# A decoder layer's first norm: its weight row by a 512 KB transfer instead of two products, and one run of warm-up products

## The chip, the cores and the metric

The kernel runs on one core of one Trainium2 chip. A core has five engines that run side by side and wait for each other by semaphores: TensorE (PE: matrix products, with a path of its own for loading weights, PEld), VectorE (DVE), ScalarE (ACT), GpSimd (POOL) and SyncE (SP), which here only issues transfers. Sixteen DMA engines move data between the main memory and the on-chip memory SBUF; TensorE writes to PSUM, a smaller memory that DVE and ACT can read.

The metric is the device time of one execution in microseconds, lower is better. The kernel before takes 733.38 us (median of 3 runs, 732.4 to 733.74).

## The reference

One layer of a hybrid decoder on 512 tokens of width 1024, all in float32. Cut to the frame, with the three mixers left as calls:

```python
def rms_norm(x, g):
    return x * lax.rsqrt(jnp.mean(x * x, axis=-1, keepdims=True) + EPS) * g

def reference(x, norm_mix, w_in, ..., w_out, norm_ffn, w_ffn1, w_ffn2):
    h = rms_norm(x, norm_mix[0])
    proj = h @ w_in[0]                        # 1024 -> 2974 columns, split into the parts below
    qkv_a, z_a, b_a, a_a, q_b, kv_b, gate_b, u_c = split_columns(proj)
    y_a = gdn_mixer(...)                      # convolution, gated delta rule in chunks of 64, 6 heads
    y_b = nsa_mixer(...)                      # compressed, selected and windowed attention, 6 heads
    y_c = pool_mixer(...)                     # causal means over 2, 4, 8 and 16 tokens
    x = x + concat(y_a, y_b, y_c) @ w_out[0]
    h = rms_norm(x, norm_ffn[0])
    return x + square(relu(h @ w_ffn1[0])) @ w_ffn2[0]
```

The change lies wholly in the first line: `norm_mix[0]` is a row of 1024 weights that every token's row of `x` is multiplied by.

## The kernel before

**Tiling.** The 512 tokens are four tiles of 128 rows, `x0` to `x3` (128 partitions by 1024 columns, 512 KB each). Every float32 product of the large projections is made of three products of rounded parts: a tile is split into `hi` (rounded, by ACT) and `lo` (the rest, by DVE), and `hi*hi`, `hi*lo` and `lo*hi` are summed in PSUM.

**The first stage** (the first 24 us or so) makes the normalised and transposed `hTh` and `hTl` out of `x`. It has these steps for tile `i`, each a function whose calls stand in the order in which they are wanted:

- `load_x(i)` (L200) loads the tile. `dma_a(0)` and `dma_a(1)` (L206) load the 286 columns of `w_in` that are projected first, in two halves of four row blocks each, `raw`.
- `norm_sq(i)` (L153): ACT squares the tile and sums each row into `ss`.
- `norm_root(i)` (L159): the reciprocal square root of the 128 sums by three Newton steps: three small DVE instructions (L163 to L165), then six more, on DVE for tile 0 (L171, L172) and on POOL for tiles 1 to 3 (L168, L169).
- `norm_b(i)` (L175): DVE forms `scr = x * r * gmix` in two halves of 512 columns (L179), `gmix` being the weight row on all 128 partitions; TensorE transposes the eight 128 by 128 blocks against the identity (L183).
- `norm_c(i)` (L186): ACT and DVE split the transposed blocks into `hTh` (L191) and `hTl` (L192).
- `hi_a`, `lo_a` (L210, L215) split the loaded columns of `w_in` (ACT, L213; DVE, L218), and `proj_a` (L250) multiplies with them (L257 to L259).

The calls from L307 to L331 give the order of all of this. `kp` (`keep_in_program_order`) marks the instructions whose order on their engine is the written one, so none of them overtakes another there: the DVE part of `norm_root(1)`, for one, is written ahead of `lo_a(0)`, which is written ahead of `norm_c(0)`.

**The weight row and the warm-up** (L224 to L240). The row is loaded as one row on one partition, `grow` (4 KB, issued by ACT). A column of ones, `onep` (1 by 128), times each half of `grow` gives a 128 by 512 PSUM tile whose rows are all that half: the two tiles `gmix`, which stay in two of the eight PSUM banks until `norm_b(3)`. Around these two products stand two runs of eight products of the identity with itself, whose result nobody reads: they keep TensorE busy before there is work for it.

**The order elsewhere.** SP issues nearly all loads, one after the other in the order of its program. After the first stage there is no written order for the engines: a scheduler plays the program through with its own estimate of durations and puts each instruction where its inputs are there first. So a change at the start can change the order of instructions that it doesn't touch. The delta rule (`gdn_solve` with products of L804; `gdn_step` with L884, L888, L901, L909), the projections (L429), the compression (L592 to L612) and the start of the attention are interleaved in this way. The last stage (the MLP) is one long run of products.

Of the kernel before, what the change touches and what calls it, by code (L numbers as in the profile page):

```python
# [9 lines left out]
F32 = mybir.dt.float32  # L10
# [10 lines left out]
P = 128  # L21
T = 512
D = 1024
# [14 lines left out]
def trunk_kernel(ctx, tc, x, norm_mix, w_in, conv_w, a_log, dt_bias, gdn_norm, nsa_q_norm, nsa_k_norm,  # L38
                 cmp_pos, cmp_w1, cmp_w2, pool_w, pool_scale, w_out, norm_ffn, w_ffn1, w_ffn2, out):
    nc = tc.nc  # L40
    V, S, G, PE, SY = nc.vector, nc.scalar, nc.gpsimd, nc.tensor, nc.sync

    def pool(name, bufs, side="left", space=None, reuse="tile"):
        kw = {} if space is None else {"space": space}
        return tc.tile_pool(name=name, bufs=bufs, side=side, reuse_waits=reuse, **kw)
# [11 lines left out]
    def banks(*ids):  # L57

        c = [0]

        def get():
            b_ = ids[c[0] % len(ids)]
            c[0] += 1
            return bank.tile([P, 512], F32, tag=f"b{b_}", name=nm("ps"))

        return get
# [4 lines left out]
    pp_, ps_, pc_ = banks(3, 6), banks(3), banks(6)  # L71

    def ctile(shape, dt, name):
        return cst.tile(shape, dt, tag=name, name=name)
# [12 lines left out]
    xin = xes.enter_context(pool("xin", 1, side="right"))  # L87

    ident = ctile([P, P], F32, "ident")
# [6 lines left out]
    def bc(ap, name, n, tmp=True):  # L96
        t = xin.tile([P, n], F32, tag=name, name=name) if tmp else ctile([P, n], F32, name)
        SY.dma_start(t, ap.partition_broadcast(P))
        return t
# [51 lines left out]
    kp = tc.keep_in_program_order  # L151
# [48 lines left out]
    def load_x(i):  # L200
        t = xin.tile([P, D], F32, tag=f"x{i}", name=f"x{i}")
        SY.dma_start(t, x[0, ts(i, P), :])
        xw[i] = t
        xt[i] = [t[:, ts(b, T)] for b in range(2)]
# [16 lines left out]
                slab_a[c].append(t_[:, k])  # L221

    xt, xw, ra, nr, nps = {}, {}, [], {}, {}
    one1 = xin.tile([1, 1], F32, tag="one1", name="one1")  # L224
    V.memset(one1, 1.0)
    S.activation(one1, one1, AF.Square)
    load_x(0)
    grow = xin.tile([1, D], F32, tag="grow", name="grow")
    S.dma_start(grow, norm_mix[0:1, :])
    onep = xin.tile([1, P], F32, tag="onep", name="onep")  # L230
    V.memset(onep, 1.0)
    wps = pn()
    gmix = [pp_() for _ in range(2)]
    for n_ in (8, None, 8):
        if n_:
            for _ in range(n_):
                kp(PE.matmul(wps[:, 0:P], ident, ident, start=True, stop=True))
        else:
            for b in range(2):
                kp(PE.matmul(gmix[b], onep, grow[:, ts(b, T)], start=True, stop=True))  # L240
    for i in range(2):
        ra.append(dma_a(i))
        load_x(i + 1)
# [1178 lines left out]
```

## Time and profile before

| | |
|---|---|
| median of 3 runs | 733.38 us (732.4 to 733.74) |
| the profiled execution | 730.48 us |
| its span, first to last instruction | 728.6 us |
| TensorE busy | 701.8 us, 96% of the span |
| VectorE, ScalarE, GpSimd busy | 557.3, 387.5, 167.4 us |
| mean granted TensorE clock | 0.988 |

All times of rows are microseconds from the start of the span. Busy time counts from an instruction's start to its modelled end. A row of the timeline shows in square brackets how long the engine had been idle before it and what ended that. The granted clock of 1.00 is 2.4 GHz and 0.50 is 1.2 GHz.

### The profile page before, as it was taken

The page shows a single profiled execution, that of the slowest core. Times are in us where ns is not written, and L with a number is a line of the kernel's source. Part 1 is how long each engine was busy: PE and PEld are TensorE (multiplying, and loading weights), DVE is VectorE, ACT ScalarE, POOL GpSimd, SP SyncE. Part 2 cuts the span into 40 slices and gives each one's busy share as a digit, 9 for nine tenths or more (in the row PEclk, how much of TensorE's full clock was granted, in tenths as well). Part 3 has the DMA queues.
Part 4 walks back from the last instruction along what each step waited for, and adds up shares of the span by engine and source line. Part 5 has one row for each costly group of instructions (what it writes and reads, how often), then busy time and mean ns, then how long its engine had stood idle before and what let it go on. Part 6 is the DMA issues. An engine that isn't in the chain of part 4 may idle for free.

```text
span 728.6 us, 13287 instructions
## 1 busy us (share of the span) xinstructions
PE 701.8 (96%) x5147; PEld 574.5 (79%) x5147; DVE 557.3 (76%) x1061; ACT 387.5 (53%) x768; POOL 167.4 (23%) x257
## 2 busy tenths in 40 slices
PE   8999999999999999899899999999999999999997
PEld 6888887887988776666678878888888888888885
DVE  6778998878686678877646798997968586796836
ACT  5455745664653558468734844545453544544430
POOL 6810012312132110000020140505032050504123
PEclk9999999998999999899999999999999999999999
DMA  6242213141400500323011152415051333312103
GB/s 221 66 131 87 74 44 89 31 110 44 126 22 16 232 1 30 95 88 109 0 38 51 59 173 94 139 58 167 14 166 58 117 115 108 124 47 70 57 1 115
DMA packets 49780, 61.67 MB, mean 85 GB/s; under 512 B 5479, under 2 KB 42549, under 8 KB 49718
## 3 DMA queue, kind: packets, MB, share of 16 engines
q1 hardware_dynamic: 48852, 60.64, 26.5%
q8 instruction: 40, 0.66, 0.4%
q10 hardware_dynamic: 866, 0.20, 0.1%
q14 instruction: 22, 0.18, 0.1%
HBM read 58.73 MB, written 2.10 MB: 83 GB/s over the span
## 4 chain that ended last, share of the span: by engine, by line
PE 71%; DVE 16%; ACT 4%; DMA 4%; issue 3%; POOL 2%; SPq 0%; DVEq 0%; ACTq 0%; POOLq 0%
PE ps L143 17%; PE ps L144 17%; PE ps L145 17%; PE ps L429 6%; PE ps L804 2%; PE ps L1144 2%; DMA raw<-in_w_ffn_dram 2%; PE ps L1130 1%; DVE lw L135 1%; DVE lo L135 1%; DMA raw<-in_w_out_dram 1%; PE ps L592 1%; PE ps L1105 1%; DVE lwo L135 1%; DVE bl L1298 1%
## 5 line engine op out<-in xcount | busy, mean ns | idle before, releaser
L144 PE MATMUL ps<-h2l,hw 128*128 128x512 f32 (+1 forms) x280 | 104.9, 375 | 0.1
L145 PE MATMUL ps<-h2h,lw 128*128 128x512 f32 (+1 forms) x280 | 104.8, 375 | 0.0
L143 PE MATMUL ps<-h2h,hw 128*128 128x512 f32 (+1 forms) x280 | 104.1, 375 | 0.0
L143 PE MATMUL ps<-bh,ah 128*128 128x512 f32 x224 | 88.3, 394 | 0.7 <-DVE x L1391 0.7
L144 PE MATMUL ps<-bl,ah 128*128 128x512 f32 x224 | 88.2, 394 | 0.0
L1305 POOL TENSOR_TENSOR al<-gF,ah 128x512 fp32r<-128x512 f32 x24 | 35.0, 1459 | 230.0 <-ACT ah L1304 190.5
L145 PE MATMUL ps<-bh,al 128*128 128x512 f32 x224 | 84.4, 393 | 0.0
L1391 DVE TENSOR_TENSOR x<-ps,x 128x512 f32<-128x512 f32 x112 | 73.1, 683 | 14.4 <-PE ps L145 14.4
L1298 DVE TENSOR_TENSOR bl<-w2r,bh 128x1024 fp32r<-128x1024 f32 x40 | 57.8, 1448 | 7.2 <-ACT bh L1297 7.2
L144 PEld LDWEIGHTS ps<-h2l,hw 128*128 128x128 f32 x280 | 52.6, 188 | 10.4 <-DVE h2l L1269 0.3
L145 PEld LDWEIGHTS ps<-h2h,lw 128*128 128x128 f32 x280 | 52.6, 188 | 10.2
L143 PEld LDWEIGHTS ps<-h2h,hw 128*128 128x128 f32 x280 | 52.3, 188 | 10.0
L1297 ACT CAST bh<-w2r 128x1024 fp32r<-128x1024 f32 x40 | 41.8, 1047 | 32.6 <-PE ps L145 32.0
L1305 POOL TENSOR_TENSOR al<-gS,ah 128x512 fp32r<-128x512 f32 x32 | 54.1, 1707 | 17.3 <-ACT ah L1304 17.3
L135 DVE TENSOR_TENSOR lo<-raw,hi 128x512 fp32r<-128x512 f32 (+1 forms) x76 | 43.9, 601 | 14.9 <-ACT hi L134 12.5
L134 ACT CAST hi<-raw 128x512 fp32r<-128x512 f32 (+1 forms) x76 | 37.0, 518 | 28.4 <-DMA raw<-in_w_in_dram 12.2
L143 PEld LDWEIGHTS ps<-bh,ah 128*128 128x128 f32 x224 | 42.1, 188 | 11.2 <-ACT ah L1304 0.9
L145 PEld LDWEIGHTS ps<-bh,al 128*128 128x128 f32 x224 | 42.1, 188 | 9.7
L144 PEld LDWEIGHTS ps<-bl,ah 128*128 128x128 f32 x224 | 42.1, 188 | 9.7
L134 ACT CAST hw<-raw 128x1024 fp32r<-128x1024 f32 x32 | 32.2, 1047 | 27.1 <-PE ps L144 23.5
L135 DVE TENSOR_TENSOR lw<-raw,hw 128x1024 fp32r<-128x1024 f32 x32 | 39.1, 1256 | 8.4 <-ACT hw L134 8.2
L144 PE MATMUL ps<-hTl,hi 128*128 128x512 f32 x104 | 41.3, 397 | 0.0
(375 smaller groups left out, 1687.1 us busy)
## 6 DMA issues: line engine op xcount, KB each, us to landing
raw<-in_w_ffn_dram SPq DMA_DIRECT2D x32, 512.0 KB, 3.8
w2r<-in_w_ffn_dram SPq DMA_DIRECT2D x32, 512.0 KB, 4.5
raw<-in_w_in_dram SPq DMA_DIRECT2D x24, 256.0 KB, 2.9
raw<-in_w_in_dram SPq DMA_DIRECT2D x36, 128.0 KB, 2.6
x<-in_x_dram SPq DMA_DIRECT2D x8, 512.0 KB, 6.3
raw<-in_cmp_w_dram SPq DMA_DIRECT2D x32, 128.0 KB, 2.1
raw<-in_w_out_dram SPq DMA_DIRECT2D x8, 512.0 KB, 4.5
out_dram<-x SPq DMA_DIRECT2D x8, 256.0 KB, 2.0
```

The lines of the kernel that those rows point to most:

```text
L134: {"A": S.copy, "V": V.tensor_copy, "G": G.tensor_copy}[e[0]](hi[:, k], r)
L135: {"V": V, "G": G}[e[1]].tensor_tensor(lo[:, k], r, f32v(hi[:, k]), ALU.subtract)
L143: PE.matmul(ps, ah, bh, start=start, stop=False, **kw)
L144: PE.matmul(ps, ah, bl, start=False, stop=False, **kw)
L145: PE.matmul(ps, al, bh, start=False, stop=stop, **kw)
L429: PE.matmul(ps[:, ts(i, 256)], a_[:, k, ts(2 * b + i, P)], w_, start=(k == 0 and n_ == 0 and i == 0), stop=(k == KC - 1 and n_ == 2 and i ...
L804: PE.matmul(ps[halves[p], ts(s_, 64)], lhsT(halves[p], s_), rhs(halves[p], s_), start=True, stop=True)
L1144: PE.matmul(acc[0:64 if b == 2 else P, i * P:(i + m) * P], v_ if b == 2 else v_.rearrange("p c d -> p (c d)"), p_[:, c * P:(c + m) * P], s ...
L1297: S.copy(hi, src)
L1298: V.tensor_tensor(lo, src, f32v(hi), ALU.subtract)
L1305: G.tensor_tensor(lo, src, f32v(hi), ALU.subtract)
L1391: V.tensor_tensor(x2[i][:, cs], acc[bk, t_], x2[i][:, cs], ALU.add)
```

## The change

The weight row is loaded straight onto all 128 partitions: `bc`, a helper that the kernel already has for small rows, issues one transfer from SP whose source is read 128 times (128 rows of 4 KB, 512 KB), right behind the load of `x0`. `gmix` is now two halves of that SBUF tile. The load of `grow` by ACT, the two products and the two PSUM banks go. `onep` becomes a 128 by 128 tile of ones, set by DVE as its first instruction, and the warm-up is one run of 22 products of it with itself.

```diff
+    onep = xin.tile([P, P], F32, tag="onep", name="onep")
+    V.memset(onep, 1.0)
     one1 = xin.tile([1, 1], F32, tag="one1", name="one1")
     V.memset(one1, 1.0)
     S.activation(one1, one1, AF.Square)
     load_x(0)
-    grow = xin.tile([1, D], F32, tag="grow", name="grow")
-    S.dma_start(grow, norm_mix[0:1, :])
-    onep = xin.tile([1, P], F32, tag="onep", name="onep")
-    V.memset(onep, 1.0)
+    gm_b = bc(norm_mix[0], "gm_b", D)
+    gmix = [gm_b[:, ts(b, T)] for b in range(2)]
+
     wps = pn()
-    gmix = [pp_() for _ in range(2)]
-    for n_ in (8, None, 8):
-        if n_:
-            for _ in range(n_):
-                kp(PE.matmul(wps[:, 0:P], ident, ident, start=True, stop=True))
-        else:
-            for b in range(2):
-                kp(PE.matmul(gmix[b], onep, grow[:, ts(b, T)], start=True, stop=True))
+    for _ in range(22):
+        kp(PE.matmul(wps[:, 0:P], onep, onep, start=True, stop=True))
```

The line numbers of the changed kernel are 5 lower than those of the kernel before from here on.

SP's program at its start, the kernel before (`x` with a number is a token tile, `raw` the columns of `w_in`, `vrow` small rows):

```order
L202 DMA x_90<-in_x_dram 128x1024
L127 DMA raw_119<-in_w_in_dram 128x4x268
L127 DMA raw_119<-in_w_in_dram 128x4x18
L202 DMA x_122<-in_x_dram 128x1024
L127 DMA raw_126<-in_w_in_dram 128x4x268
L127 DMA raw_126<-in_w_in_dram 128x4x18
L202 DMA x_129<-in_x_dram 128x1024
```

and the changed one:

```order
L202 DMA x_92<-in_x_dram 128x1024
L98 DMA gm_b<-in_norm_mix_dram 128x1024
L127 DMA raw_121<-in_w_in_dram 128x4x268
L127 DMA raw_121<-in_w_in_dram 128x4x18
L202 DMA x_124<-in_x_dram 128x1024
L127 DMA raw_128<-in_w_in_dram 128x4x268
L127 DMA raw_128<-in_w_in_dram 128x4x18
L202 DMA x_131<-in_x_dram 128x1024
```

One transfer of the size of a token tile stands between `x0` and all that follows on SP; nothing else moves there.

TensorE's program some 169 us into the span, where its order first differs behind the start, the kernel before (L603 belongs to the compression, L804 and L612 to the solve and the compression, L888 and L901 to one step of the delta rule's scan, L429 to a projection):

```order
L603 MATMUL ps_1985<-id_146,hid_2674 128x64 x2
L888 MATMUL ps_3098<-S_3096,kr 64x64
L804 MATMUL ps_2108<-LT_880,kr 64x64 x12
L804 LDWEIGHTS L_1401
L804 MATMUL ps_2169<-W_556,L_1401 64x64
...
L612 MATMUL ps_1985<-w_2672,hh_2678 64x64 x2
L888 MATMUL ps_3098<-S_3096,kr 64x64 x2
L554 MATMUL ps_3793<-ident,X_3737 128x128
```

and the changed one:

```order
L883 MATMUL ps_3100<-S_3098,kr 64x64 x3
L598 MATMUL ps_1987<-id_148,hid_2676 128x64 x2
L799 MATMUL ps_2110<-LT_882,kr 64x64 x12
L799 LDWEIGHTS L_1403
L799 MATMUL ps_2171<-W_558,L_1403 64x64
...
L896 MATMUL ps_3100<-vn_3107,qr 64x64 x3
L607 MATMUL ps_1987<-w_2674,hh_2680 64x64 x2
L424 MATMUL ps_3832<-hi_3833,hTh 128x256
```

The three products of the scan step (L888, here L883) now stand together and ahead of those of the compression, and the next ones of the scan (L901, here L896) follow a solve round later. From here to the first attention head's values, at about 313 us of the span before, the order of TensorE, DVE, ACT and POOL differs in many places; before and after that stretch it is the same instruction by instruction, but for the lines of the diff.

## Rows read from the trace of the kernel before

**Rows 1.** The page: busy time by engine, share of the span, instructions.
```profile
PE 701.8 (96%) x5147; PEld 574.5 (79%) x5147; DVE 557.3 (76%) x1061; ACT 387.5 (53%) x768; POOL 167.4 (23%) x257
```
**Rows 2.** Windows: length, busy PE, PEld, DVE, ACT, POOL, clock, DMA share, GB/s.
```profile
0.00:24.00 24.00, 19.90 (x118) 16.22 (x119) 15.67 (x39) 12.99 (x26) 16.83 (x75) 1.00 0.53 170
24.00:166.00 142.00, 139.36 (x1404) 116.69 (x1403) 121.38 (x299) 82.95 (x188) 30.12 (x65) 1.00 0.31 83
166.00:314.00 148.00, 138.97 (x1740) 116.28 (x1740) 110.81 (x324) 83.72 (x219) 26.61 (x44) 0.94 0.22 71
```
**Rows 3.** Chain that ended last, first 24 us: start, length, what.
```profile
9.06 0.07 DVE ss L163
...
14.08 1.41 DVE scr L179 x2
...
21.84 0.73 DVE scr L179
```
**Rows 4.** Timeline: start, length, engine, line, what, idle before and its end.
```profile
6.48 1.14 ACT L213 CAST hi<-raw 128x1144 fp32r<-128x1144 f32 x1 [0.95 <-DMA raw<-in_w_in_dram]
...
7.77 1.06 ACT L156 ACTIVATE sq<-x 128x1024 f32<-128x1024 f32 x1 [0.15 <-DMA x<-in_x_dram]
...
8.97 0.15 DVE L163 TENSOR_SCALAR ss<-ss 128x1 f32<-128x1 f32 x1
```
**Rows 5.** Windows of the transfers: length, clock, DMA share, GB/s.
```profile
10.00:11.00 1.00, 1.00 1.02 407
```
**Rows 6.** Windows and packets while the small rows are spread over the partitions.
```profile
12.40:13.00 0.60, 1.00 0.25 61
...
DMA packets 53, 0.04 MB, mean 61 GB/s; under 512 B 5, under 2 KB 53, under 8 KB 53
...
13.40:14.40 1.00, 1.00 0.08 20
```
**Rows 7.** Groups by line and form, DVE: busy, mean ns, idle before.
```profile
L179 DVE SCALAR_TENSOR_TENSOR scr<-x,r,ps 128x512 f32<-128x512 f32 x8 | 5.6, 743 | 1.0 <-POOL r L169 0.9
...
L500 DVE SCALAR_TENSOR_TENSOR acc<-th,acc 128x512 f32<-128x512 f32 x9 | 6.2, 688 | 1.1 <-ACT th L499 1.0
...
L1373 DVE TENSOR_TENSOR gS<-gF 128x512 f32<-128x512 f32 x8 | 12.0, 1504 | 0.0
```
**Rows 8.** Timeline, POOL and DVE, around the roots of tiles 1 and 3.
```profile
9.42 1.35 DVE L218 TENSOR_TENSOR lo<-raw,hi 128x1144 fp32r<-128x1144 f32 x1
9.60 1.39 POOL L168 TENSOR_SCALAR rs<-r,ss 128x1 f32<-128x1 f32 x1 [1.74 <-DVE r L165]
...
18.38 1.41 DVE L179 SCALAR_TENSOR_TENSOR scr<-x,r,ps 128x512 f32<-128x512 f32 x2 [0.33 <-POOL r L169]
...
18.76 0.26 POOL L169 TENSOR_SCALAR r<-rs,r 128x1 f32<-128x1 f32 x1
...
20.37 0.26 POOL L169 TENSOR_SCALAR r<-rs,r 128x1 f32<-128x1 f32 x1
...
20.56 1.34 DVE L192 TENSOR_TENSOR hTl<-ps,hTh 128x512 fp32r<-128x512 f32 x2 [0.78 <-ACT hTh L191]
```
**Rows 9.** Timeline: the warm-up, the first transposes, SP's next load, its use.
```profile
1.78 3.78 PE L237 MATMUL ps<-ident 128*128 128x128 f32 x16 [1.78 <-POOL ident masks.py:199]
...
7.43 2.05 PE L237 MATMUL ps<-ident 128*128 128x128 f32 x16
...
9.32 1.04 PE L183 MATMUL ps<-ident,scr 128*128 128x128 f32 x8
...
13.54 1.25 SPq L127 DMA_DIRECT2D raw<-in_w_in_dram  x2
...
24.14 1.14 ACT L134 CAST hi<-raw 128x512 fp32r<-128x512 f32 x2
```
**Rows 10.** Windows, PE alone: length, busy, clock, DMA share, GB/s.
```profile
170.00:176.30 6.30, 5.93 (x69) 0.50 0.07 14
...
293.00:302.00 9.00, 6.66 (x40) 1.00 0.46 120
```

## The prediction, made before the changed kernel was run

> **What bounds the kernel now.** I read the busy times first: TensorE is busy 96% of the span [rows 1], so what a change is worth is what it does to the stretches in which TensorE is not fed. The windows by stage come next [rows 2]. From 24 to 166 us TensorE is busy 139.4 of 142 us: a delay at the start goes through this stretch undiminished, since nothing there waits long enough to take it up. From 166 to 314 us it is idle 9.0 us of 148 and the clock averages 0.94. In the first 24 us, where the change lies, it is idle 4.1 us, and much of what counts as busy is warm-up. What sets the end there is seen in the chain of waits [rows 3]: not products, but the run square, root, `scr`, next root on ACT, DVE and POOL, tile after tile, up to the last `scr` at 21.84; TensorE starts its unbroken run after the transposes of that. The timeline shows the link that matters here [rows 4]: ACT's square of `x1` starts at 7.77, after 0.15 us of waiting for the transfer, and DVE takes its sum at 8.97, while `scr` of tile 0 ends on DVE at 9.06 [rows 3, 4]. The two arrive together, so a later `x1` has no slack to hide in.
>
> **The transfer.** `gm_b` is 128 rows of 4 KB, 524,288 bytes, issued second on SP, ahead of the columns of `w_in` and of `x1`. The DMA engines are full in this stretch: with the same 4 KB rows they carry 407 GB/s at a share of 1.02 [rows 5], so whatever stands behind `gm_b` comes 524,288 / 407,000 = 1.29 us later. The trace has no spread of that size, so I bound it. Below: nothing, if the engines found room elsewhere; the share of 1.02 speaks against that. Above: the spread of a small row of 768 bytes runs at 61 GB/s [rows 6], which would make it 8.6 us. But in those 0.6 us 53 packets start at a share of only 0.25, and the 256-byte rows a little later make 20 GB/s at 0.08 [rows 6]: 88 and 78 packets per us. The pace there goes by packets and not by bytes, and 128 packets at 88 per us are 1.45 us. I take 1.3 us, with 0 and 8.6 kept as ends.
>
> **What it delays.** `raw` of the first half lands just ahead of 6.48 [rows 4], now 7.78; ACT's 1.14 us on it end at 8.92. `x1` is there at 7.77 + 1.3 = 9.07, its sum at 8.97 + 1.3 = 10.27. Behind that sum on DVE stand, in written order, the rest of DVE's part of tile 1's root, `lo_a(0)` and `hTl` of tile 0; POOL's part of the root waits for it too, so TensorE's first projection and `scr` of tile 1 (14.08 [rows 3]) move with it: +1.3 us. `x2`, `x3` and the second half of `w_in` are later by the same 1.3 us as their users. Their users were not waiting for them, so they add nothing. `gm_b` itself stands ahead of `raw` and so lands before 7.78. `scr` of tile 0 starts at 9.06 - 1.41 = 7.65 now; even if it waited for 7.78 it would be done by 9.2, and DVE has nothing to do after it until 10.27. So its landing is hidden. The small rows and the next `w_in` load (issued at 13.54, used at 24.14 [rows 9]) hide behind the stage.
>
> **What it saves.** The two products and the load of `grow` were done when the root was, so taking them away moves no start of `scr`. What stays of it: `scr` now reads both tensors from SBUF. With one in PSUM a half takes 743 ns; a line of the same kind with both in SBUF takes 688 [rows 7]. Five halves lie on the chain behind the late sum (two of tile 1, two of tile 2, the first of tile 3): 5 x 0.055 = 0.3 us off.
>
> **DVE against POOL.** A DVE instruction with two SBUF inputs and a POOL instruction get in each other's way: POOL's step at 9.60 takes 1.39 us and ends with DVE's `lo_a(0)`, begun at 9.42, while the same kind of step takes its normal time beside `scr` of tile 2 (0.26 us at 18.76) as long as that reads PSUM [rows 8]. After the change it doesn't. Held back for all of `scr` from 18.76, POOL's root of tile 3 would end some 1.04 us later than now (20.37 + 0.26 = 20.63), at 21.67; the last `scr` is behind `hTl` of tile 2, which ends at 20.56 + 1.34 = 21.90 [rows 8]. That cover is thin but holds. The other way round, DVE may wait for a POOL step: between 0 and, by a 512-column line that runs beside POOL all the time (1504 ns for some 690 [rows 7]), 2 x 0.8 = 1.6 us. Only a few 0.3 us steps meet `scr` here, so I take 0.2 us.
>
> The Trainium skill (SBUF — State Buffer, section "SBUF: two separate sides") states this as a lock: a DVE instruction with two SBUF inputs and a GpSimd instruction exclude each other for the whole instruction. The trace agrees at 9.60 [rows 8]. By this rule taken strictly, a POOL step that runs when `scr` is due holds it for the step's 0.3 us, and the sum below would be 1.3 in place of 1.2.
>
> **The warm-up.** Now: 16 passes in 3.78 us, that is 0.236 each, later 16 passes in 2.05, 0.128 each [rows 9]; that is the half and the full clock, though the windows give 1.00 for both. TensorE starts at 1.78 because it waits for the identity; the ones are set by DVE, which is free then, so it starts sooner, I guess at 1.1. 22 products are 44 passes: if the clock rises at about the same time (5.5), 19 slow and 25 fast ones, 4.5 + 3.2 us, an end at 8.8; as the first half of `scr` is ready at 7.65 + 0.74 = 8.4, the transposes come 0.5 us sooner than at 9.32 [rows 9]. It is worth nothing, because `hTl` of tile 0 now stands on DVE behind the late sum. It has a price instead: TensorE has almost nothing to do from about 9.8 (8.8 + 1.04, end of the transposes) to 12.1 (end of `lo_a(0)`, 9.42 + 1.35 + 1.3 [rows 8]). I cost that at 0 and treat a falling clock as a rival.
>
> **The order from 166 to 314 us.** It differs there on four engines, by the scheduler's own estimate. Both orders hold the same instructions, so the price is a difference of waits. Before, the stretch loses 9.0 us to idle time and 148 x 0.06 = 8.9 us to the clock [rows 2]. I can't tell from the order which one waits less: the three products of a scan step come together and earlier, which helps the chain of the scan, but the waits ahead of the compression stay and less independent work stands between two scan steps. The largest single event of the stretch is 6.3 us at half clock [rows 10], worth 3.2 us; one more or one fewer of these bounds the term, -3.2 to +3.2, and I take 0, in the middle.
>
> **Sum.** 1.3 - 0.3 + 0.2 + 0 + 0 = +1.2 us on the profiled execution: 730.48 becomes 731.7, its span 729.8. The profiled execution lies 2.9 us under the median of the runs, 733.38; the same +1.2 there gives 734.6.
>
> **Rivals.**
> 1. The new order waits less: one half-clock spell of the size in [rows 10] goes, -3.2 + 1.2 = -2.0: 731.4. For it: the scan runs ahead. Against: nothing in the change aims at it. 17%.
> 2. The new order waits more, slower than forecast: +3.2 + 1.2 = +4.4, 737.8. 18%.
> 3. The clock falls in the idle spell between warm-up and first projection. For it: in the kernel before, 9.0 us in which TensorE is busy 6.7 stand before another half-clock spell [rows 10]. Against: the first 24 us hold idle spells as well and products kept full speed. Its price: if 13 of the first projection's 24 products run at half speed and lose what a pass lost in [rows 9], 0.236 - 0.128 = 0.11 us each, that is 1.4 us, of which the wait for `lo_a(1)`, later as well, hides a part, I take 0.4: +1.0, so 735.6. 10%. The Trainium skill (TensorE: Matmul & The Clock Gate, section "HAM oscillation") has the rule behind this: gaps without products put the engine back to half rate, and the next work starts slow. No row here shows it in this place.
> 4. The spread is slow: at the 61 GB/s of [rows 6] `x1` comes 8.6 us later and, as `scr` of tile 0 waits too, all follows: +8.6 - 0.3 + 0.2 = +8.5, 741.9. Against: its pace goes by packets. 7%.
> 5. The delay is not there: `x1` comes no later, or the waits of 166 to 314 us take it up, 733.4, no change. 10%.
>
> **How the numbers follow.** 38% is left for the forecast, 734.6, whose own range is 733.9 to 736.0 (the transfer 1.3 to 1.45, the lock 0 to 1.6, small shifts of order). What a measurement can tell from no change is about 0.2%, 1.47 us: from 731.9 to 734.85. The forecast case lies at that edge, and I split it evenly, 19 and 19. Slower: these 19, 16 of rival 2 and 7 of rival 3 (the rest of both being smaller than priced), and the 7 of rival 4: 49%. Faster: 13 of rival 1, and 2 of rival 5 where some gain is left: 15%. The same: the remaining 36%. The range reaches from 731.0, below the first rival, to 739.0, above the second, and leaves out the fourth.
>
> **What would show it.** Right: ACT's square of `x1` starts near 9.1 after waiting for its transfer, DVE is idle before the sum of tile 1 until 10.3, the last `scr` starts near 23.0, and the 24 to 166 us stretch is as full as before. The halves of `scr` take about 690 ns where POOL is idle. Wrong: a square of `x1` at 7.8; a `scr` of tile 0 that waits for `gm_b`; products of the first projection 0.24 us apart; or a difference that arises behind 166 us, in the idle time or the clock, and outweighs the start.

## The result, and the profile after

The changed kernel takes 724.61 us (median of 5 runs, 724.29 to 725.93), the kernel before in the same job 733.38 us (728.6 to 735.64): a ratio of 0.9896, 95% interval 0.987 to 0.9922. In a second job the same two kernels gave 0.992 (0.9899 to 0.9941). The forecast was 734.6, slower; the range began at 731.0. The profiled execution takes 724.29 us, its span is 722.5 us.

The page and the windows of the changed kernel, columns as in [rows 1] and [rows 2]:

```profile
PE 696.9 (96%) x5155; PEld 573.0 (79%) x5155; DVE 554.8 (77%) x1061; ACT 386.4 (53%) x768; POOL 170.6 (24%) x257
...
0.00:24.00 24.00, 19.73 (x112) 18.09 (x113) 13.51 (x35) 11.75 (x21) 14.99 (x54) 0.93 0.59 189
24.00:166.00 142.00, 139.13 (x1374) 116.92 (x1374) 121.12 (x295) 83.11 (x192) 33.17 (x85) 1.00 0.30 81
166.00:314.00 148.00, 140.42 (x1820) 117.06 (x1817) 114.75 (x339) 88.11 (x229) 27.51 (x44) 0.99 0.24 76
```

Against [rows 2] two windows moved. The first 24 us now hold a spell at a lower clock (0.93); in 166 to 314 us the clock is 0.99 in place of 0.94, and 80 more products fit in; but that window does not hold the same work in both. To see where the 6.2 us of the profiled executions come from, the instructions of DVE and ACT were paired between the two traces by source line and count, and the start in one trace subtracted from that in the other. The changed kernel is 2.4 us behind at 24 to 40 us, 1.8 behind at 140 to 160, 6.2 ahead at 320, and 6.1 ahead at the end. So the start lost time, as forecast, and one stretch won 7.9 us. That 2.4 us become 1.8 is no sign of slack in between: a second trace of the kernel before (e5 below) gains 0.7 us on the first over the same work.

**The start.** The timeline of the changed kernel, in the order of [rows 4]:

```profile
4.82 1.06 ACT L156 ACTIVATE sq<-x 128x1024 f32<-128x1024 f32 x1 [2.52 <-DMA x<-in_x_dram]
...
8.52 1.15 ACT L213 CAST hi<-raw 128x1144 fp32r<-128x1144 f32 x1 [2.55 <-DMA raw<-in_w_in_dram]
...
9.81 1.06 ACT L156 ACTIVATE sq<-x 128x1024 f32<-128x1024 f32 x1
...
10.99 0.15 DVE L163 TENSOR_SCALAR ss<-ss 128x1 f32<-128x1 f32 x1 [1.49 <-ACT sq L156]
...
19.25 1.29 DVE L192 TENSOR_TENSOR hTl<-ps,hTh 128x512 fp32r<-128x512 f32 x2 [1.17 <-ACT hTh L191]
...
20.23 0.26 POOL L169 TENSOR_SCALAR r<-rs,r 128x1 f32<-128x1 f32 x1
...
20.91 1.42 DVE L179 SCALAR_TENSOR_TENSOR scr<-x,r,gm_b 128x512 f32<-128x512 f32 x2
...
21.08 1.30 POOL L168 TENSOR_SCALAR rs<-r,ss 128x1 f32<-128x1 f32 x1 [0.58 <-DVE r L165]
...
22.84 0.34 POOL L168 TENSOR_SCALAR rs<-r,ss 128x1 f32<-128x1 f32 x1
...
24.39 1.41 DVE L179 SCALAR_TENSOR_TENSOR scr<-x,r,gm_b 128x512 f32<-128x512 f32 x2
```

The chain of waits that ended last, in the same stretch (start, length, what, as in [rows 3]):

```profile
2.73 7.00 DMA x<-in_x_dram
...
9.81 1.16 ACT sq L156 x2
...
24.09 0.27 POOL r L169
...
24.39 0.76 DVE scr L179
```

The cast of the first columns of `w_in` waits for its transfer until 8.52 (6.48 before, [rows 4]) and keeps ACT until 9.67. `x1` lands at 2.73 + 7.00 = 9.73, and its square starts 0.08 us behind that, at 9.81 (7.77 before). The timeline shows no wait there because ACT had been free for 0.14 us only, but the chain goes by the transfer. The sum of tile 1 comes at 10.99 (8.97), the last `scr` at 24.39 (21.84, [rows 3]). TensorE in the same stretch, and one window of it (columns as in [rows 10]):

```profile
1.12 8.13 PE L235 MATMUL ps<-onep 128*128 128x128 f32 x44 [1.12 <-DVE one L227]
...
9.08 1.13 PE L183 MATMUL ps<-ident,scr 128*128 128x128 f32 x8
...
11.48 0.40 PE L252 MATMUL ps<-hi,hTh 128*128 128x286 f32 x1 [1.27 <-ACT hTh L191]
...
12.85 0.40 PE L253 MATMUL ps<-lo,hTh 128*128 128x286 f32 x1 [0.97 <-DVE lo L218]
...
14.20:17.50 3.30, 3.30 (x16) 0.50 0.12 32
```

After the transposes TensorE has nothing to do but one product until 12.85, and from about 14.2 to 17.6 it runs at 1.2 GHz.

**166 to 314 us.** The stretch between the same instructions is 166 to 314 us in the kernel before and 167.76 to 307.85 in the changed one:

```profile
167.76:307.85 140.09, 132.51 (x1738) 110.77 (x1739) 109.17 (x327) 83.38 (x219) 27.51 (x44) 0.99 0.23 74
```

With [rows 2] beside it: 148.0 us became 140.1; TensorE's busy time fell from 138.97 to 132.51 (6.5 us), its idle time from 9.0 to 7.6 (1.5 us). The work is the same, so the busy time fell because less of it ran at half clock: 17.1 us of the stretch before, 3.4 us in the changed kernel, in the clock of the two traces. The timeline of TensorE at the first place where the order differs and at a later one, some of the rows with a wait in front, first the kernel before and then the changed one:

```profile
167.02 0.38 PE L804 MATMUL ps<-TT,R 64*64 64x64 f16 x12 [0.49 <-DVE R L849]
...
167.82 0.39 PE L429 MATMUL ps<-hi,hTh 128*128 128x256 f32 x1 [0.43 <-DVE qks L542]
...
169.18 0.91 PE L603 MATMUL ps<-id,hid 128*128 128x64 f32 x4 [0.43 <-ACT hid L600]
...
229.46 0.38 PE L804 MATMUL ps<-TT,R 64*64 64x64 f16 x12 [1.39 <-DVE R L849]
```

```profile
164.59 0.38 PE L799 MATMUL ps<-TT,R 64*64 64x64 f16 x12 [0.30 <-DVE R L844]
...
171.22 0.45 PE L607 MATMUL ps<-w,hh 128*64 128x64 f32 x4 [0.35 <-DVE hh L603]
...
227.09 0.92 PE L799 MATMUL ps<-X,LT 64*64 64x64 f32 x24 [0.51 <-DVE TT L853]
...
228.40 0.91 PE L799 MATMUL ps<-LT,kr 64*64 64x64 f32 x24 [0.39 <-DVE LT L860]
```

Before, three waits stand within 2.6 us, and the clock is halved right behind them; a single wait of 1.39 us at 228 stands ahead of another half-clock spell. In the new order the waits at these two places are shorter and further apart, and in this trace no spell follows until 287 us.

### The profile page after: what moved, and what is told of

The parts are those of the page before. It is cut to its first block, busy times and chain, and to the rows that moved or that the text cites. A ratio compares the mean times of both kernels' runs of the same rounds, so it can differ in the third digit from the quotient of the medians.

```text
span 722.5 us, 13307 instructions
## 1 busy us (share of the span) xinstructions
PE 696.9 (96%) x5155; PEld 573.0 (79%) x5155; DVE 554.8 (77%) x1061; ACT 386.4 (53%) x768; POOL 170.6 (24%) x257
## 4 chain that ended last, share of the span: by engine, by line
PE 71%; DVE 16%; ACT 4%; DMA 4%; issue 3%; POOL 1%; SPq 0%; DVEq 0%; ACTq 0%; POOLq 0%
PE ps L143 17%; PE ps L144 17%; PE ps L145 17%; PE ps L424 5%; PE ps L799 2%; PE ps L1139 2%; PE ps L1125 1%; DMA raw<-in_w_in_dram 1%; PE ps L587 1%; DVE lw L135 1%; DMA raw<-in_w_ffn_dram 1%; DMA x<-in_x_dram 1%; PE ps L1100 1%; DVE bl L1293 1%; DVE lwo L135 1%
## 5 line engine op out<-in xcount | busy, mean ns | idle before, releaser
L1386 DVE TENSOR_TENSOR x<-ps,x 128x512 f32<-128x512 f32 x112 | 72.9, 681 | 10.6 <-PE ps L145 10.5
L1299 ACT CAST ah<-gS 128x512 fp32r<-128x512 f32 x32 | 19.8, 621 | 45.1 <-DVE gS L1368 24.5
```

What stands on the lines that cost most here:

```text
L1299: S.copy(hi, src)
L1386: V.tensor_tensor(x2[i][:, cs], acc[bk, t_], x2[i][:, cs], ALU.add)
```

## The experiments

All kernels below differ from one of the two in the lines shown and in nothing else that behaves differently (where the loop of the kernel before is changed, the spreading products read `onep[0:1, :]`, the same row). Behind the start each has the order, on all engines, of the kernel that is named with it: the number, the place or the operand of the warm-up products is enough to make the scheduler choose another order. Theory A: the order of 166 to 314 us made the gain, and the transfer only costs. Theory B: the transfer and the warm-up made it. Theory C: half-clock spells come and go by execution. Times are medians; ratios are to the kernel before in the same job, with 95% intervals.

**The same order with the other start.** The start of the kernel before, with the changed kernel's order:

```diff
-    for n_ in (8, None, 8):
+    for n_ in (10, None, 8):
```

> The start of the kernel before (row of weights on one partition, two spreading products, identity warm-up), with 10 + 8 instead of 8 + 8 warm-up products. Behind the start its order is that of the changed kernel, on every engine. Theory A (the order of 166 to 314 us made the gain, the transfer only costs): the changed kernel's 724.6 less the 1.8 us by which its start is behind at 160 us, 722.8; one half-clock spell or none in 166 to 314 us. Theory B (transfer and warm-up make the gain): as before, 733.4. Theory C (half-clock spells come and go by execution, whatever the order): anywhere between 723 and 735, its spells not those of the changed kernel.

The changed kernel with the order of the kernel before (the tile of ones and its setting by DVE, no longer used, go too, so TensorE starts at 1.78 as before):

```diff
-        kp(PE.matmul(wps[:, 0:P], onep, onep, start=True, stop=True))
+        kp(PE.matmul(wps[:, 0:P], ident, ident, start=True, stop=True))
```

> The changed kernel with one thing different: its 22 warm-up products multiply the identity and not the tile of ones. Behind the start its order is that of the kernel before, on every engine. Theory A: 733.4 + 1.8 (start) = 735.2, with three or four half-clock spells in 166 to 314 us, the long one near 170 us among them. Theory B: 724.6 to 726. Theory C: anywhere between 723 and 737.

Measured: 723.62, ratio 0.9893 (0.9864 to 0.9923), and 733.3, ratio 1.0019 (1.0 to 1.0038). The gain went with the order and not with the transfer: theory B fell. In the second trace the half-clock spells are those of the kernel before, each about 3.4 us later, as its start is. Windows inside these four spells, the kernel before and then the changed start with the old order (length, busy PE, clock, DMA share, GB/s):

```profile
169.50:176.20 6.70, 6.33 (x66) 0.50 0.08 19
230.90:234.20 3.30, 3.10 (x14) 0.50 0.00 0
289.00:292.20 3.20, 3.13 (x11) 0.50 0.47 164
302.60:305.90 3.30, 3.30 (x9) 0.50 0.33 134
```

```profile
172.90:179.60 6.70, 6.28 (x69) 0.50 0.07 15
234.30:237.60 3.30, 3.15 (x14) 0.50 0.00 0
292.30:295.70 3.40, 3.33 (x12) 0.50 0.53 154
306.00:309.30 3.30, 3.30 (x9) 0.50 0.27 108
```

Theory C in its plain form fell with them.

**One product more or less; four less; ones for the identity.** The kernel before with `(8, None, 9)`, `(8, None, 7)`, `(4, None, 8)` in the same line, and with the 128 by 128 tile of ones as the operand of its warm-up. Four more orders.

> The kernel before with one more warm-up product (8 + 9), which ends before the transposes begin and so delays nothing. Behind the start its order is a third one, which differs from both kernels in some 680 of TensorE's 5550 entries. Theory A: another time than 733.4 by more than 1.5 us, its sign unknown, made behind 166 us. Theory B: 733.4, within 0.7.

> The kernel before with one warm-up product less (8 + 7). Behind the start its order is a fourth one (some 610 of TensorE's entries differ from before, 710 from the changed kernel). Theory A: a time of its own again, different from that of the run with one more by over 1.5 us as likely as not, and the difference arises behind 166 us. Theory B: 733.4, within 0.7.

> The kernel before with 4 + 8 instead of 8 + 8 warm-up products. A fifth order behind the start, the nearest to that of the kernel before so far (some 260 of TensorE's entries differ). Theory A (the order decides): a time between the two kernels or beyond them, within 2 us of 731.4 if only the differing entries near 170 us matter little; its start may lose up to 1 us where the clock has not risen in time. Theory B (the start decides): 731.4 to 732.4.

> The kernel before with one part of the change alone: the warm-up (8, the two spreading products, 8) multiplies a 128 by 128 tile of ones set by DVE, the row is spread by products as before. A sixth order behind the start (some 500 of TensorE's entries differ from before, 620 from the changed kernel). Theory A: a time of its own between 722 and 738, made in 166 to 314 us. Theory B (the transfer makes the gain): 731.4 within 0.7; if the operand of the warm-up made it: 724.

Measured: 731.6, 1.0001 (0.9972 to 1.0031); 737.69, 1.0074 (1.0051 to 1.0096); 735.94, 1.0051 (1.0023 to 1.0079); 733.83, 1.0021 (0.9995 to 1.0047). One warm-up product taken away, which can only let TensorE go on sooner, made the kernel 0.74% slower; in its trace 3.4 us of that arise in the stretch, and 3.1 us at the start. (The expectation of one product more called it free. It is not: the warm-up stands in front of the first transposes, which begin at 9.32 in [rows 9] though half of their `scr` is there at 8.4.) Of the nine-product kernel theory A had expected a time of its own; its stretch was 2.1 us faster, but its start 4.2 us behind (below), so its time came out as before's. For the nearest order (`4, None, 8`) theory A had allowed 2 us; it was 4, of which its trace has 2.1 in the stretch and 2.3 at the start. The last one shows that the clock is not all of it:

```profile
166.00:314.00 148.00, 136.25 (x1776) 0.97 0.23 72
```

This is TensorE's window in the kernel with the ones: a better clock than the 0.94 of [rows 2], yet 148.00 - 136.25 = 11.75 us idle in place of 9.0, and the stretch 1.0 us slower.

**The kernel before, two more traces.** Unchanged.

> The kernel before, unchanged, for a second trace of it. Its executions differ in mean granted clock (0.984 to 0.997) and in time (730 to 737). Theory A1 (the old order loses by its half-clock spells): an execution with fewer such spells in 166 to 314 us is faster by half of what they no longer last, so with 7 instead of 17 us of them by 5 us. Theory A2 (the old order loses by what its engines wait for one another, and the clock falls because TensorE waits): the time stays within 1.5 us of 730.5 whatever the clock, and the idle time of TensorE in the stretch grows by what the spells give back.

> The kernel before, unchanged, a third trace. As for the second one: theory A1 5 us faster for 10 us less of half clock, theory A2 the same time within 1.5 us and more idle time of TensorE in place of the slow time.

Measured: 730.09 and 734.23 us. Neither execution had few enough spells to part A1 from A2. The second lacks the last spell of the kernel before; across that place it makes up 1.3 us on the first trace (paired instructions: 4.9 us behind at 280 to 300, 3.6 past it). Where a spell of 6.8 us stood in place of one of 3.4, or beside none, in two traces of one kernel (the runs f6 and g2 below), it cost 1.7 and 2.5 us more. So a microsecond at half clock cost some 0.36 to 0.5 us here, an estimate from three places. The stretch of the kernel before has 17.1 us of it and that of the changed kernel 3.4: 4.9 to 6.8 of the 7.9 us are clock, by this estimate, the rest shorter waits. No run kept the old order and its waits and changed the clock alone; that split stays an estimate.

The second trace showed something else, which the profile of the forecast had not: its start is 3.8 us behind that of the first, in the same kernel.

```profile
1.79 3.78 PE L237 MATMUL ps<-ident 128*128 128x128 f32 x16 [1.79 <-POOL ident masks.py:199]
5.50 3.78 PE L240 MATMUL ps<-grow,onep 1*128 1x512 f32 x4
9.21 3.78 PE L237 MATMUL ps<-ident 128*128 128x128 f32 x16
12.78 1.74 PE L183 MATMUL ps<-ident,scr 128*128 128x128 f32 x8
```

All warm-up passes take 0.236 us here, where those from 7.43 on took 0.128 in [rows 9]. The spreading products take 3.78 us, and the second run of warm-up products, in written order ahead of the first transposes, holds these back to 12.78; in [rows 9] they start at 9.32. The other traces bear this out. In nine traces with the spreading products and a long warm-up the first transposes begin at 9.32, 9.47, 10.53, 11.07, 12.12, 12.35, 12.78, 13.21 and 13.63 us, and the start is behind by 0, 0.2, 1.5, 2.3, 2.9, 3.1, 3.8, 4.2 and 4.1 us. The long warm-up costs most in just those executions in which it does not raise the clock in time. The Trainium skill (TensorE: Matmul & The Clock Gate, section "Part 1: The HAM clock gate (the 'warmup' mystery)") says that the number of slow products at a kernel's start differs from run to run of one kernel; these two traces agree.

**The parts of the new start, in the new order.** The changed kernel with no warm-up products, with 16, with the row's transfer one place later, and the start of the kernel before with `(9, None, 9)`:

```diff
-    for _ in range(22):
+    for _ in range(0):
```

> The changed kernel without its 22 warm-up products; its order is otherwise that of the changed kernel on every engine, and the output is the same. Theory W (the warm-up decides whether TensorE's clock rises at 5 to 7 us or only at 13 to 15 us, and a late rise costs the 3.7 us by which one trace of the kernel before is behind another): 724.6 + 3.5 = 728, in all executions alike. Rival (the first stage hangs on square, root and scr, so a slow TensorE is hidden): 724.6 within 0.7.

> The changed kernel with 16 warm-up products instead of 22, the number of the kernel before, in one run; order otherwise as in the changed kernel. Theory W: executions of two kinds, near 724.6 and near 728, as the kernel before has them near 730.5 and 735.5; the spread of the times is over 3 us, where the changed kernel's was 1.6. Rival (22 products are no better than 16, the narrow spread was chance or the order's): 724.6, spread below 2 us.

```diff
-    gm_b = bc(norm_mix[0], "gm_b", D)
-    gmix = [gm_b[:, ts(b, T)] for b in range(2)]
...
     for i in range(2):
         ra.append(dma_a(i))
+        if i == 0:
+            gm_b = bc(norm_mix[0], "gm_b", D)
+            gmix = [gm_b[:, ts(b, T)] for b in range(2)]
         load_x(i + 1)
```

> The changed kernel with its 512 KB row transfer issued behind the first half of the columns of w_in instead of ahead of it; the order is otherwise that of the changed kernel on every engine. Theory T (the transfer costs what it pushes back): the cast of the first columns starts near 6.5 instead of 8.52, the square of x1 near 9.1 behind its own transfer instead of 9.81 behind the cast, so the first sum of tile 1 comes 0.6 to 0.7 us sooner: 724.0. Rival T2 (it shares the engines with its neighbours wherever it stands): 724.6 within 0.3, the cast no sooner than 7.5.

> The start of the kernel before with 9 + 9 instead of 8 + 8 warm-up products; behind the start the order of the changed kernel again. Theory A: as the first such kernel, 722.8, faster than the changed kernel by 1 to 2.6 us in executions whose clock rises at 5 to 6 us, about 3.5 us more in the others. Theory B: 731.4.

Measured: 725.11, 0.9906 (0.9883 to 0.9929); 725.56, 0.9916 (0.9894 to 0.9939); 725.98, 0.9914 (0.9889 to 0.9939); 725.31, 0.9916 (0.9894 to 0.9938). Theory W fell: without any warm-up the time is the same, and with 16 products the executions lie within 2.4 us, where it had said over 3 (and its rival below 2). It is not the missing warm-up that costs, but one that stands in front of the transposes. Theory T fell as well. The timeline of the kernel with the row one place later:

```profile
6.33 1.15 ACT L213 CAST hi<-raw 128x1144 fp32r<-128x1144 f32 x1 [0.73 <-DMA raw<-in_w_in_dram]
...
9.37 1.41 DVE L179 SCALAR_TENSOR_TENSOR scr<-x,r,gm_b 128x512 f32<-128x512 f32 x2 [1.78 <-DMA gm_b<-in_norm_mix_dram]
...
10.62 1.06 ACT L156 ACTIVATE sq<-x 128x1024 f32<-128x1024 f32 x1 [3.15 <-DMA x<-in_x_dram]
```

The cast comes at 6.33, as theory T had it, but `scr` of tile 0 now waits 1.78 us for the row, and the square of `x1` waits for its transfer until 10.6 instead of 9.1. Theory T took that square to have stood behind the cast in the changed kernel; by the chain above it stood behind its own transfer there too, and `x1` is behind the row at either place. Moving the row won nothing: ahead of the columns its transfer puts their cast back by 2.0 us, behind them `scr` waits 1.8 us for it. The last one agrees with theory A's order, not with its 722.8: its start was in the late kind (4.1 us behind).

**A start with hardly any warm-up, four orders.** The kernel before with no warm-up products ahead of the spreading ones and 3, 4, 5 or 6 behind them:

```diff
-    for n_ in (8, None, 8):
+    for n_ in (0, None, 4):
```

> The same start with 3 products behind the spreading ones; the order is that of the kernel with 8 + 7 products, whose stretch was 3.4 us slower than that of the kernel before. Order theory: 730.5 + 3.4 = 733.9. Start theory: as the one with 4 products.

> The kernel before with no warm-up products ahead of the two spreading products and 4 behind them; its order is otherwise that of the kernel before on every engine. Theory S (the long warm-up costs the kernel before 3.7 us in those executions in which the clock rises late, because it then stands in front of the transposes): all executions near 730.5, none above 732.5, the median about 1 us under the kernel before's. Rival (the warm-up is needed: without it the first projections run at half clock): 733 or more.

> The same start with 5 products behind the spreading ones; the order is that of the kernel with 8 + 9 products, whose stretch was 2.1 us faster than that of the kernel before. Order theory: 730.5 - 2.1 = 728.4. Start theory (the order carries nothing): as the one with 4 products.

> The same start with 6 products behind the spreading ones; behind the start the order of the changed kernel on every engine. By the stretch of 166 to 314 us, which that order runs 7.7 to 9.1 us faster in six traces: 730.5 - 8.5 = 722.0, faster than the changed kernel (724.6) by the 1.8 to 2.6 us of its transfer. If the transfer or the long run of products is a part of the gain: no faster than 724.6.

Measured: 734.01, 1.0009 (0.9987 to 1.003); 730.6, 0.9972 (0.9946 to 0.9997); 729.22, 0.9957 (0.9931 to 0.9983); 724.03, 0.9867 (0.9835 to 0.9898). The forecasts from the stretches were 733.9, 730.5, 728.4 and 722.0: the sequence is right, the last 2 us too fast. From 4 to 6 products, with nothing else changed in the source, is 1.1% (0.9867 / 0.9972 = 0.9895), as much as the whole change under study. Three of the 12 executions with 4 products lie above the 732.5 of theory S (732.6 to 733.46), none at 736 as before's. So its bound of 732.5 was missed.

**The transfer alone, in one job.** The changed kernel again, and the one with 6 products again:

> The changed kernel once more, beside the other start with the same order. By its first runs 0.9896 of the kernel before.

> The two spreading products and 6 warm-up products behind them, with the order of the changed kernel, in the same job as the changed kernel. If the transfer costs the 1.8 us by which the changed kernel's start is behind at 160 us: 1.8 us faster than the changed kernel's runs beside it, 0.9871 of the kernel before. If the start is taken up by what follows: the same within 0.7 us.

Measured: 725.44, 0.992 (0.9899 to 0.9941), and 726.32, 0.9924 (0.9896 to 0.9951). The 1.8 us that the transfer was to cost did not show; the rival, "the same within 0.7", is nearer, though the medians are 0.9 us apart the other way. The second one's trace, of the slowest of its six executions (728.3), is 2.2 us ahead of the changed kernel's at 140 to 160 us, yet loses it behind: two spells of 6.8 us at half clock that the changed kernel's trace lacks.

```profile
242.00:248.60 6.60, 6.46 (x36) 0.50 0.99 374
320.40:327.10 6.70, 6.35 (x16) 0.50 0.25 79
```

So theory C keeps this much: within one order an execution can lose some 4 us by its spells (the 1.7 and 2.5 above). What the transfer costs at the end is too small to be seen beside that. No version here was shown to beat the changed kernel: 0.9867 and 0.9924 are the same file in two jobs.

**All traces together.** Start: us behind the first trace of the kernel before at 24 to 40 us. Stretch: change of that between 140 to 160 and 320 to 340 us. Clock: of the window 166 to 314 us.

| start | order | run: start, stretch, clock |
|---|---|---|
| 8, row, 8 | old | before: 0, 0, 0.94; e5: 0.2, +0.1, 0.94; e6: 3.8, -0.4, 0.95 |
| 0, row, 4 | old | f4: 0.3, +2.0, 0.94 |
| transfer, 22 | old | e2: 3.6, -0.4, 0.94 |
| transfer, 22 | new | after: 2.4, -7.9, 0.99; g1: 2.9, -8.8, 1.00 |
| transfer, 0; 16; row later | new | e9: 2.7, -9.1, 1.00; e10: 3.5, -8.0, 1.00; e11: 4.4, -7.7, 0.99 |
| 10, row, 8; 9, row, 9 | new | e1: 1.5, -8.7, 0.99; e12: 4.1, -9.1, 1.00 |
| 0, row, 6 | new | f6: 0.3, -7.3, 0.99; g2: 0.8, -2.6, 0.98 |
| 8, row, 9; 0, row, 5 | third | e3: 4.2, -2.1, 0.95; f5: 0.9, -2.0, 0.95 |
| 8, row, 7; 0, row, 3 | fourth | e4: 3.1, +3.4, 0.95; f3: -0.2, +5.7, 0.95 |
| 4, row, 8; 8, row, 8 with ones | two more | e7: 2.3, +2.1, 0.97; e8: 2.9, +1.0, 0.97 |

The stretch goes by the order: -0.4 to +2.0 in five traces of the old one, -2.6 to -9.1 in nine of the new one, eight of these beyond -7. The ninth, g2, has its second spell at 320.4 to 327.1, behind the stretch, in work whose order is the same in all; paired at 306 to 320 us, ahead of that spell, its change is -6.4. The traces of f3, f4, e11 and g2 are of the slowest execution of their kernels. Two window rows for it, TensorE alone, the old order with the short start and the new one without warm-up:

```profile
166.00:314.00 148.00, 137.50 (x1749) 0.94 0.22 71
```

```profile
166.00:314.00 148.00, 140.58 (x1828) 1.00 0.24 76
```

## Why the prediction was wrong

**The order, 0 with bounds of -3.2 to +3.2: the step that failed.** It is the term that was mis-sized: -7.9 us in the profiled execution. The bound was built on the largest single half-clock spell. Nothing in the rows said that only one spell could go; [rows 2] gave 8.9 us as the loss to the clock and 9.0 as idle time, and a better order could win back a part of both. How much a worse order could lose, no row said. Rival 1, "the new order waits less", had the mechanism and its first piece, the spell of [rows 10], but priced one spell, where four became one (17.1 us at half clock became 3.4) and the idle time shrank by 1.5 us too. The order's price is not peculiar to this change: the other orders, from one warm-up product more or less, moved the stretch by -2 to +6 us.

**The transfer, +1.3.** Right in kind: the sum of tile 1 came at 10.99, 2.0 us later in place of 1.3. Two things differ from the sum. The rate of 407 GB/s was that of 10 to 11 us [rows 5]; from 2 to 8 us the engines carried 332 GB/s before and 311 after (the last column; first the kernel before), which makes 524,288 / 311,000 = 1.7 us. And `x0`, issued ahead of the row, is itself 0.44 us later (its square starts at 4.82, 4.38 before); how much of the other 0.3 us comes from that was not shown. The link held as forecast: the square of `x1` starts behind its own transfer, 2.04 us later than before. Rival 4, the slow spread, did not occur.

```profile
2.00:8.00 6.00, 6.00 (x25) 4.53 (x26) 2.07 (x10) 3.38 (x6) 5.24 (x27) 1.00 1.00 332
```

```profile
2.00:8.00 6.00, 6.00 (x33) 6.00 (x33) 1.72 (x9) 1.44 (x4) 5.25 (x27) 1.00 1.00 311
```

**`scr` from SBUF, -0.3.** Wrong. The halves take 749 ns, 743 before [rows 7]; the 688 of the other line did not carry over.

```profile
L179 DVE SCALAR_TENSOR_TENSOR scr<-x,r,gm_b 128x512 f32<-128x512 f32 x8 | 5.7, 749 | 1.0 <-POOL r L169 1.0
```

**DVE against POOL, +0.2.** The lock is there, and where it was looked for: POOL's step at 21.08 takes 1.30 us beside `scr` at 20.91, as the one at 9.60 in [rows 8]; alone such a step takes 0.34. Its cover was used up: POOL's root of tile 3 ends at 24.36 and `hTl` of tile 2 leaves DVE free for the `scr` at 24.39, and the chain goes by POOL; the sum had 0.2 us between the two (21.67 and 21.90). As the Trainium skill has it (SBUF — State Buffer, section "SBUF: two separate sides"), one of the two is blocked for the whole instruction; the trace agrees. It cost next to nothing.

**The warm-up, 0, and rival 3.** The end was forecast at 8.8 and the run starts at 1.12 and ends near 9.25; the clock did fall in the gap behind it, as rival 3 had it (10%). The transposes of tile 1 stand at 18.00, one us after the first half of their `scr`. `hTl` of tile 1 waits for them until 19.25 and holds up the `scr` of tile 2 behind it on DVE until 20.91, while POOL's root for it was done at 20.49: the 0.4 of the rival. The last `scr` is 2.55 us behind where the sum was 2.0. The Trainium skill (TensorE: Matmul & The Clock Gate, section "HAM oscillation") has the rule that gaps without products put the engine back to half rate and the next work starts slow. The trace agrees with the first half, behind idle times of 1.27 and 0.97 us, and not quite with the second: five more products ran at full speed from 12.85 on before the clock fell near 14.2.

**What the sum left out.** The start at 140 to 160 us is 1.8 us behind, +1.2 forecast: near enough. But the zero of that sum was one execution. Of eight further traces with the spreading products and a long warm-up seven begin 1.5 to 4.2 us behind it, and the six with the transfer 2.4 to 4.4: against a usual start of the kernel before, the change costs little. How many executions begin late in a job would also make the difference of the medians vary (8.8 us in the first job, 5.0 in the second, 6.2 between the profiled executions); that was not shown for each execution.

**Chances.** Faster had 15%; the case for it was seen and its size not.

## What to carry to other kernels

Where a scheduler orders the engines by its own estimates, an edit at the start can also be a new order far behind it: compare the orders first, and test the edit with the order held (here two warm-up products more or less, or another operand for them, switch between the old order and the new) before the edit gets the credit or the blame. Bound the price of a new order by all that the stretch loses to waits and to the clock, not by one event. And a warm-up run in front of real work is paid at half clock whenever the clock rises late; read the start from more than one trace.

## What was not expected of the hardware

- The clock rose before 7.4 us in one trace of the kernel before and not before its warm-up had ended at 13 us in another, with the same products issued (passes of 0.128 and 0.236 us); the two differ by 3.8 us at 24 us.
- The changed kernel without any warm-up lost nothing that could be measured: 725.11 against 724.61 and 725.44.
- A DVE product of three operands, 128x512 float32, takes 0.74 to 0.75 us whether its second tensor is in PSUM or in SBUF.
- In the old order half-clock spells nearly kept their places in the work: in e2, e5 and e6, whose work was moved by up to 4.9 us, they begin within 1 us of them. In f4 the first begins 4.7 us later in the work, and e6 lacks the last. A microsecond in them cost some 0.36 to 0.5 us, by the estimate above.
